# x staged in eight buffers, squares summed on VectorE, and columns of scales turned into rows on TensorE

## The chip, the cores and the metric

The kernel runs on one core of one Trainium2 chip. The metric is device time in microseconds (us), the median of several runs; lower is better. Engine names are those of the profile: PE is TensorE (PEld its weight load), DVE VectorE, ACT ScalarE, POOL GpSimd, and SP the engine that issues nearly all DMAs, in the order of its instructions.

## The reference

The reference is one layer of a hybrid encoder on x, 1024 tokens of width 1024, in float32:

```python
h = rmsnorm(x, norm_g[l])                 # x * rsqrt(mean(x*x) + eps) * g
u = h @ w_in[l]                           # 1024 -> 5312 columns, split for the three mixers and a gate
y_conv = conv_module(...)                 # GLU, depthwise conv of 31 taps, LayerNorm, SiLU
y_ret  = retention_branch(...)            # 4 heads, two directions, chunks of 128
y_mla  = mla_branch(...)                  # rmsnorm of two latents, 8 heads, dense softmax attention
y = jnp.concatenate([y_conv, y_ret, y_mla], axis=-1) * jax.nn.silu(u_gate)
x = x + y @ w_out[l]
return rmsnorm(x, final_g)
```

Four scales are a mean over the width turned into one number per token: rsqrt of the mean square of x, of the query latent and of the key-value latent, and rsqrt of the conv's variance. The softmax sums are one number per token and head.

## The kernel before

Activations lie with features on the 128 partitions and tokens along a row. Each matrix product is made of three matmuls of split operands (high part times high, low times high, high times low: lines 175 to 177, helper `mm3`). A Python program issues work in an order of its own, and a scheduler of the framework then interleaves the streams; each engine runs its instructions in one fixed order, and SP's DMA issues too.

**Prologue (0 to 60 us).** `load_x` brings x in 8 tiles of 128 x 1024 (k = 0 to 7) into tag `hp`, which has four buffers; ACT makes the high part xH, DVE the low part xL (line 63, inside `split_l`), and PE multiplies them with the first weight unit. `sq_x` squares a tile in place on ACT and adds it to the sum `cm` (the tile `ssx`): six adds on POOL, the last on DVE (`SQD`). So the tile of k = 4 to 7 comes in only when the add of k - 4 has freed its buffer.

**Scales of tokens.** `row_rsqrt` (four calls: `cm`, `lss`, `lsk`, `va`) sums over the partitions with eight matmuls of one column against ones (line 300). The stationary operand there takes every eighth token, `ss.rearrange("p (q n) -> p n q", n=KT)[:, n, :]`, so that token p*8 + n ends at partition p, column n. DVE scales the 128 x 8 column (line 301), POOL takes the power (302), SP writes it to memory (303: `r_dram`, `lq_dram`, `lk_dram`, `cr_dram`) and reads it back on all partitions as a row (305, `rbc` for x). For x a column layout `rcol` is read back too (308). PE runs on meanwhile with the next projection unit; the results of the units wait in PSUM for `rbc`, since DVE's evictions multiply by it.

**Projections, conv, retention (60 to 540 us).** PE runs projection units back to back; DVE does the evictions, the weight splits and the 31 conv taps.

**Attention (540 to 990 us).** 16 units (8 heads by two halves of the tokens). A unit makes scores S (lines 810 to 814), row maxima on DVE (817), exponentials with their sums `rs` on ACT (819), transposes of P on PE into the PSUM tag `pp`, which has two banks (828), a copy and a split of them (830, 63), and P times V (175 to 177). `Unit.norm` (833 to 842) takes reciprocals of the 128 x 4 tile `rs`, writes it to memory with `rs_dram<-rs` (839), reads it back as a row on all partitions (841, `rb`) and multiplies the gate with it on POOL. Between the units stand the preparation of the next heads: loads of their weights (`wr`, line 643), the rope turn `xs<-xr` (759), and, late, the output weights `wor` and `yr` (923, 935) for the output projection.

Of the kernel before, what the change touches and what calls it, by code (L numbers as in the profile page):

```python
# [13 lines left out]
ADD, SUB, MUL, MAX = ALU.add, ALU.subtract, ALU.mult, ALU.max  # L14

P = 128
S = 1024
D = 1024
KT = D // P
HS = 512  # L20
CONV_K = 31
HALO = CONV_K // 2
# [8 lines left out]
EPS = 1e-6  # L31
# [14 lines left out]
T18, T19 = 8, 8  # L46
XN = [4, 1, 1, 1, 1, 1, 1, 1]
LASTC = [(0, 0, 256), (1, 0, HS), (0, 256, HS)]
SQD = (7,)
W2_BUFS = 11  # L50
NWARM = 12

# [4 lines left out]
def body(tc, xT, x, w_in, w_uqn, w_uqr, w_uk, w_uv, w_out, vecs, decay, final_g,  # L57
         t_ret, t_mla, t_idx, t_iota, idm, out):
    nc = tc.nc
    act, dve, pool, pe, sp = nc.scalar, nc.vector, nc.gpsimd, nc.tensor, nc.sync  # L60
# [4 lines left out]
    def tt(eng, o, a, b, op):  # L65
        eng.tensor_tensor(o, a, b, op=op)  # L66

    def split_l(eng, lo, src, hi, scale=1.0):
        stt(eng, lo, src, scale, hi.bitcast(F32), MUL, SUB)

    root = ExitStack()
    const = root.enter_context(tc.tile_pool(name="const", bufs=1, side="left"))
# [5 lines left out]
    def ps(tag, w=HS):  # L78
        cnt[0] += 1
        return psp[0].tile([P, w], F32, name=f"ps{cnt[0]}", tag=tag, bufs=PSB[tag])  # L80
# [3 lines left out]
    rr = {"m": 0, "b": 0}  # L84
# [5 lines left out]
    def ps_bg():  # L90
        rr["b"] += 1
        return ps(BG[rr["b"] % len(BG)])

    def mk(pl, shape, dt=F32, tag=None, bufs=None):
        cnt[0] += 1
        kw = {} if bufs is None else {"bufs": bufs}
        return pl.tile(shape, dt, name=f"{tag}{cnt[0]}", tag=tag, **kw)

    r_dram = tc.dram_tile([S], F32, name="r_dram")
# [5 lines left out]
    rcol = mk(const, [P, KT], tag="rcol")  # L105
# [3 lines left out]
    ones = mk(const, [P, P], tag="ones")  # L109
# [11 lines left out]
    rbc = mk(p1, [P, S], tag="rbc")  # L121
# [4 lines left out]
    cv = cvx.enter_context(tc.tile_pool(name="cv", bufs=1, side="right"))  # L126

    ssx = mk(cv, [P, S], tag="cm")

    def load_x(k, n):  # L130
        tf = mk(cv, [P, S + 2 * HALO], tag="hp", bufs=4)[:, :S]
        g = vec[:, V_G + k:V_G + k + 1]
        for i in range(n):
            c = slice(i * S // n, (i + 1) * S // n)
            sp.dma_start(tf[:, c], xT[k * P:(k + 1) * P, c])
            if k == 0 and i == 0:
                pool.dma_start(vec, vecs)
                w0[0][2](0, 1)
            act.activation(xH[k][:, c], tf[:, c], AF.Identity, scale=g)  # L139
            split_l(dve, xL[k][:, c], tf[:, c], xH[k][:, c], g)  # L140
        xraw.append(tf)

    def sq_x(k):
        tf = xraw[k]
        if k == 0:
            act.activation(ssx, tf, AF.Square)
        else:
            act.activation(tf, tf, AF.Square)
            tt(dve if k in SQD else pool, ssx, ssx, tf, ADD)

    xraw = []

    def load_w(u, g, steps=()):
        hi = mk(p1, [P, 4, UW], F32R, tag="wh", bufs=4)
        lo = mk(p1, [P, 4, UW], F32R, tag="wl", bufs=4)
        t = mk(p1, [P, 4, UW], tag="wraw", bufs=2)

        def piece(a, b):
            sp.dma_start(t[:, a:b], w_in[u, g, :, a:b])
            act.copy(hi[:, a:b], t[:, a:b])  # L160
            split_l(dve, lo[:, a:b], t[:, a:b], hi[:, a:b])

        if steps is None:
            return hi, lo, piece
        sp.dma_start(t, w_in[u, g])
        act.copy(hi, t)  # L166
        split_l(dve, lo, t, hi)
        return hi, lo
# [5 lines left out]
    def mm3(o, sh, sl, mh, ml, first, last, skip=False):  # L174
        pe.matmul(o, sh, mh, start=first, stop=False, skip_group_check=skip)  # L175
        pe.matmul(o, sh, ml, start=False, stop=False, skip_group_check=skip)  # L176
        pe.matmul(o, sl, mh, start=False, stop=last, skip_group_check=skip)  # L177
# [88 lines left out]
    for k in range(KT):  # L266
        if k % 4 == 0:
            w0.append(load_w(0, k // 4, None))
        if k == 1:
            w0[0][2](1, 2)  # L270
        elif k > 0 and k % 2 == 0:
            w0[k // 4][2](k % 4, k % 4 + 2)
        load_x(k, XN[k])
        wh, wl = w0[k // 4][0][:, k % 4, :], w0[k // 4][1][:, k % 4, :]
        n = S // 4 if XN[k] == 4 else HS
        for h in range(2):
            for c in range(0, HS, n):
                for t in range(2):
                    c0 = h * HS + c
                    mm3(o4[2 * t + h][:, c:c + n], wh[:, t * P:(t + 1) * P], wl[:, t * P:(t + 1) * P],  # L280
                        xH[k][:, c0:c0 + n], xL[k][:, c0:c0 + n], k == 0 and c == 0, k == KT - 1, True)
        if k > 0:
            sq_x(k - 1)
    sq_x(KT - 1)
    dve.tensor_scalar(cwh, vec[:, V_CW:V_CB], 0.5, None, op0=MUL)
    wn = load_unit(1)

    hps, accs = [], []
    for i in range(NC_CONV):
        hp = mk(cv, [P, S + 2 * HALO], tag="hp", bufs=4)  # L290
# [2 lines left out]
        hps.append(hp)  # L293
        accs.append(mk(cv, [P, S], tag="acc", bufs=4))

    def row_rsqrt(ss, scale, eps, o, d):
        col = mk(const, [P, KT], tag="rrc", bufs=2)
        c = ps_bg()
        for n in range(KT):
            pe.matmul(c[:, n:n + 1], ss.rearrange("p (q n) -> p n q", n=KT)[:, n, :], ones[:, 0:1], start=True, stop=True)  # L300
        dve.tensor_scalar(col, c[:, :KT], scale, eps, op0=MUL, op1=ADD)  # L301
        pool.tensor_tensor(col, col, eps_c[:, :KT], op=ALU.pow)
        sp.dma_start(d.rearrange("(p n) -> p n", n=KT), col)
        if o is not None:
            sp.dma_start(o, d.rearrange("(o s) -> o s", o=1).to_broadcast([P, S]))

    row_rsqrt(ssx, 1.0 / D, EPS, rbc, r_dram)
    sp.dma_start(rcol, r_dram.rearrange("(t p) -> p t", p=P))
    dec = mk(const, [P, 8], tag="dec")
    sp.dma_start(dec, decay.to_broadcast([P, 8]))  # L310
    lg = mk(const, [P, 8], tag="lg")
# [33 lines left out]
    def conv_post():  # L345
        for h in range(2):
            hs = slice(h * HS, (h + 1) * HS)
            o = ps_bg()
            pe.matmul(o, ones, cm[:, hs], start=True, stop=True)
            yield  # L350
            for ci in range(NC_CONV):
                stt(dve, accs[ci][:, hs], o, -1.0 / 512.0, accs[ci][:, hs], MUL, ADD)
                if ci == 0:
                    act.activation(va[:, hs], accs[ci][:, hs], AF.Square)
                else:
                    sq = mk(cv, [P, HS], tag="cb", bufs=2)
                    act.activation(sq, accs[ci][:, hs], AF.Square)
                    tt(dve, va[:, hs], va[:, hs], sq, ADD)
                yield
        row_rsqrt(va, 1.0 / 512.0, EPS, cm, cr_dram)  # L360
        yield
        for ci in range(NC_CONV):
            a = accs[ci]
            tt(dve, a, a, cm, MUL)
            act.activation(a, a, AF.Silu, scale=vec[:, V_LG + ci:V_LG + ci + 1],
                           bias=vec[:, V_LB + ci:V_LB + ci + 1])
            yield
            for h in range(2):
                hs = slice(h * HS, (h + 1) * HS)
                g = mk(cv, [P, HS], tag="cb", bufs=2)  # L370
                sp.dma_start(g, g_dram[ci][:, hs])
                tt(dve, a[:, hs], a[:, hs], g, MUL)
            sp.dma_start(y_dram[ci], a)
            yield
# [42 lines left out]
    def trig(pl, tag):  # L417
        c, s_ = mk(pl, [P, S], tag=tag, bufs=2), mk(pl, [P, S], tag=tag, bufs=2)
        sp.dma_start(c, t_ret[0])
        sp.dma_start(s_, t_ret[1])  # L420
        tt(pool, c, c, rbc, MUL)
        tt(pool, s_, s_, rbc, MUL)
        return c, s_
# [48 lines left out]
    kT[1], qT[1] = mk(rt, [P, 2, S], tag="k1"), mk(rt, [P, 2, S], tag="q1")  # L472
    vN[1] = mk(rt, [P, NCH, UW], tag="v1")
    tr1 = trig(rt, "b4")
    ident = mk(const, [P, P], tag="ident")
    sp.dma_start(ident, idm[0])

    def w2():
        return mk(rt, [P, HS], tag="w2", bufs=W2_BUFS)
# [185 lines left out]
    def half(i):  # L665
        return slice(i * HS, (i + 1) * HS)
# [26 lines left out]
    for h in range(2):  # L693
        t, tk = mk(lx, [P, HS], tag="kr", bufs=2), mk(fin, [P, HS], tag="g" if h else "osb", bufs=2)
# [13 lines left out]
    at = atx.enter_context(tc.tile_pool(name="at", bufs=1, reuse_waits="tile", side="left"))  # L708
# [85 lines left out]
    class Unit:  # L794
# [38 lines left out]
        def norm(self):  # L833
            i = self.h * 2 + self.qh
            self.g = mk(fin, [P, HS], tag="g", bufs=2)
            sp.dma_start(self.g, g_dram[8 + self.h][:, half(self.qh)])
            dve.reciprocal(self.rs, self.rs)
            d = tc.dram_tile([HS], F32, name=f"rs_dram{i}")
            sp.dma_start(d.rearrange("(t p) -> p t", p=P), self.rs)
            rb = mk(fin, [P, HS], tag="rb", bufs=1)  # L840
            sp.dma_start(rb, d.rearrange("(o s) -> o s", o=1).to_broadcast([P, HS]))
            tt(pool, self.g, self.g, rb, MUL)
# [64 lines left out]
    for u in range(NUN):  # L907
# [33 lines left out]
        for i in range(8):  # L941
            cur.qk(i)
            t, j = (i // 2 - 1) % 4, i % 2
# [203 lines left out]
```

## Time and profile before

| | us |
|---|---|
| median of 3 runs | 1168.31 (1164.31 to 1168.86) |
| the profiled execution | 1162.01, span 1160.2 |
| PE busy | 1115.4 (96%) |
| DVE busy | 729.8 (63%) |
| ACT busy | 408.2 (35%) |
| POOL busy | 171.3 (15%) |
| mean granted clock | 0.984 |

PE carries the span. The time that it doesn't work lies in a few places, and a busy PE is slower where the granted clock is below 1, so the profile is read by stage: how much PE idles there, at which clock it runs, and which wait ended last. SP has no busy time of its own; what counts there is the moment at which it issues a DMA.

### The profile page before, as it was taken

How to read it: one execution, taken by the hardware profiler on the slowest of the kernel's cores; microseconds unless marked ns; L12 is line 12 of the kernel's file. 1: busy time of each engine (PE TensorE's matmuls, PEld its weight loads, DVE VectorE, ACT ScalarE, POOL GpSimd, SP SyncE). 2: the span in 40 equal slices, each digit the busy share in tenths (PEclk: the TensorE clock that was granted, in tenths of full speed). 3: DMA queues.
4: the chain of work that ended last, by engine and by line, in shares of the span. 5: the costliest groups of instructions: out<-in, count | busy, mean ns of one | idle time of the engine just before them, and what ended most of it. 6: DMA issues, size and time to landing. Idle time of an engine off the chain costs nothing. (4 is left out here: it accounts for less than half of the span.)

```text
span 1160.2 us, 14263 instructions
## 1 busy us (share of the span) xinstructions
PE 1115.4 (96%) x5548; PEld 933.9 (80%) x5548; DVE 729.8 (63%) x998; ACT 408.2 (35%) x721; POOL 171.3 (15%) x147
## 2 busy tenths in 40 slices
PE   7999999999999999998899999899999979999997
PEld 6888888888898899886678787688778857888886
DVE  6699999997647785746765564555455553345033
ACT  6221222121334134223654453454454443333022
POOL 4300000212220442023201101010110000001000
PEclk9999999998999999999999999999999999999999
DMA  7212223221262122226212212121211242654213
GB/s 261 92 37 73 91 83 117 87 86 46 73 227 91 46 73 69 88 72 227 86 17 74 47 43 53 35 50 35 51 52 29 31 133 56 227 172 150 68 36 109
DMA packets 55491, 101.33 MB, mean 87 GB/s; under 512 B 15584, under 2 KB 19440, under 8 KB 55424
## 3 DMA queue, kind: packets, MB, share of 16 engines
q1 hardware_dynamic: 55376, 100.35, 27.6%
q8 instruction: 43, 0.70, 0.4%
q14 instruction: 24, 0.20, 0.1%
q0 software_dynamic: 48, 0.08, 0.1%
HBM read 74.14 MB, written 24.17 MB: 85 GB/s over the span
## 5 line engine op out<-in xcount | busy, mean ns | idle before, releaser
L176 PE MATMUL ps<-xL,wh 128*128 128x512 f32 (+1 forms) x612 | 240.2, 393 | 3.2 <-DVE xL L63 3.0
L177 PE MATMUL ps<-xH,wl 128*128 128x512 f32 (+1 forms) x612 | 239.6, 392 | 1.9 <-DVE wl L63 1.9
L175 PE MATMUL ps<-xH,wh 128*128 128x512 f32 (+1 forms) x612 | 238.9, 396 | 2.2 <-ACT xH L139 1.6
L63 DVE SCALAR_TENSOR_TENSOR acc<-hp,cwh,acc 128x1024 f32<-128x1024 f32 x120 | 153.3, 1317 | 0.3 <-DVE rrc L301 0.2
L176 PEld LDWEIGHTS ps<-xL,wh 128*128 128x128 f32 x612 | 116.6, 190 | 27.6 <-DVE xL L63 4.2
L177 PEld LDWEIGHTS ps<-xH,wl 128*128 128x128 f32 x612 | 116.1, 190 | 26.5 <-DVE wl L63 2.6
L175 PEld LDWEIGHTS ps<-xH,wh 128*128 128x128 f32 x612 | 116.0, 190 | 26.6 <-ACT xH L139 1.8
L63 DVE SCALAR_TENSOR_TENSOR PL<-ps,PH 128x512 fp32r<-128x512 f32 x128 | 85.7, 685 | 48.7 <-ACT PH L830 48.4
L175 PE MATMUL ps<-woH,yh 128*128 128x512 f32 (+1 forms) x264 | 99.2, 389 | 7.6 <-ACT yh L936 7.4
L176 PE MATMUL ps<-woL,yh 128*128 128x512 f32 (+1 forms) x264 | 101.4, 387 | 0.0
L177 PE MATMUL ps<-woH,yl 128*128 128x512 f32 (+1 forms) x264 | 100.3, 387 | 0.0
L830 ACT CAST PH<-ps 128x512 fp32r<-128x512 f32 x128 | 72.6, 590 | 69.9 <-PE ps L828 69.3
L817 DVE TENSOR_REDUCE nm<-ps 128x1 f32<-128x1024 f32 x64 | 78.1, 1221 | 29.8 <-PE ps L814 29.3
L819 ACT ACTIVATE P<-ps,nm 128x1024 f32<-128x1024 f32 x64 | 71.8, 1122 | 26.3 <-DVE nm L817 24.8
L828 PE MATMUL ps<-ident,P 128*128 128x128 f32 x512 | 73.2, 274 | 4.6 <-DVE PL L63 4.5
L828 PEld LDWEIGHTS ps<-ident,P 128*128 128x128 f32 x512 | 61.5, 141 | 18.0 <-DVE PL L63 6.9
L166 ACT CAST wh<-wraw 128x1024 fp32r<-128x1024 f32 x40 | 42.1, 1051 | 95.0 <-PE ps L176 92.1
L66 POOL TENSOR_TENSOR g<-g,rb 128x512 f32<-128x512 f32 x16 | 20.6, 1289 | 362.2 <-DMA rb<-rs_dram 201.4
L175 PEld LDWEIGHTS ps<-woH,yh 128*128 128x128 f32 x264 | 49.7, 188 | 19.2 <-ACT yh L936 8.4
L63 DVE SCALAR_TENSOR_TENSOR wl<-wraw,wh 128x1024 fp32r<-128x1024 f32 (+2 forms) x45 | 55.4, 1232 | 8.2 <-ACT wh L166 7.4
L177 PEld LDWEIGHTS ps<-woH,yl 128*128 128x128 f32 x264 | 49.7, 188 | 10.8 <-DVE yl L63 0.7
L176 PEld LDWEIGHTS ps<-woL,yh 128*128 128x128 f32 x264 | 49.7, 188 | 10.4
(280 smaller groups left out, 2056.9 us busy)
## 6 DMA issues: line engine op xcount, KB each, us to landing
wraw<-in_w_in_dram SPq DMA_DIRECT2D x40, 512.0 KB, 3.4
wor<-in_w_out_dram SPq DMA_DIRECT2D x16, 512.0 KB, 4.5
g_dram<-ga SPq DMA_DIRECT2D x29, 256.0 KB, 2.0
yr<-y_dram SPq DMA_DIRECT2D x18, 256.0 KB, 4.7
g<-g_dram SPq DMA_DIRECT2D x16, 256.0 KB, 3.4
rb<-rs_dram SPq DMA_DIRECT2D x16, 256.0 KB, 4.9
y_dram<-osb SPq DMA_DIRECT2D x16, 256.0 KB, 2.4
z<-in_x_dram SPq DMA_DIRECT2D x8, 512.0 KB, 3.7
```

What stands on the lines that cost most here:

```text
L63: eng.scalar_tensor_tensor(o, a, s, b, op0=op0, op1=op1)
L66: eng.tensor_tensor(o, a, b, op=op)
L166: act.copy(hi, t)
L175: pe.matmul(o, sh, mh, start=first, stop=False, skip_group_check=skip)
L176: pe.matmul(o, sh, ml, start=False, stop=False, skip_group_check=skip)
L177: pe.matmul(o, sl, mh, start=False, stop=last, skip_group_check=skip)
L817: dve.tensor_reduce(nm, self.S, axis=AX.X, op=MAX, negate=True)
L819: act.activation(p, self.S, AF.Exp, bias=nm, accum_out=self.rs[:, t:t + 1])
L828: pe.transpose(o[:, c * P:(c + 1) * P], self.p[t][:, (4 * j + c) * P:(4 * j + c + 1) * P], ident)
L830: act.copy(ph, o)
```

## The change

1. Tiles k = 4 to 7 of x are staged in tag `acc` (four buffers that the conv uses later), so eight buffers hold the eight tiles. All seven square-adds go to DVE, and the program issues the squares after the loop of loads and splits.
2. `row_rsqrt` takes 128 tokens that lie next to each other as the stationary operand, so the column n holds tokens n*128 to n*128 + 127. The 128 x 8 column is transposed on PE into another part of the same PSUM bank, ACT copies the 8 x 128 result to SBUF, and SP writes 8 rows of 512 bytes instead of 128 of 32. `rcol` is the column itself; its read is gone. The identity for the transposes is loaded at the start.
3. `Unit.norm` transposes `rs` on PE into a `pp` bank, ACT copies the 4 x 128 result, and SP writes 4 rows of 512 bytes instead of 512 elements of 4 bytes.

```diff
     def load_x(k, n):
-        tf = mk(cv, [P, S + 2 * HALO], tag="hp", bufs=4)[:, :S]
+        tf = mk(cv, [P, S + 2 * HALO], tag="hp", bufs=4)[:, :S] if k < 4 else mk(cv, [P, S], tag="acc", bufs=4)
...
             act.activation(tf, tf, AF.Square)
-            tt(dve if k in SQD else pool, ssx, ssx, tf, ADD)
+            tt(dve, ssx, ssx, tf, ADD)
...
-        if k > 0:
-            sq_x(k - 1)
-    sq_x(KT - 1)
+    for k in range(KT):
+        sq_x(k)
...
-    def row_rsqrt(ss, scale, eps, o, d):
-        col = mk(const, [P, KT], tag="rrc", bufs=2)
+    def row_rsqrt(ss, scale, eps, o, d, col=None):
+        if col is None:
+            col = mk(const, [P, KT], tag="rrc", bufs=2)
         c = ps_bg()
         for n in range(KT):
-            pe.matmul(c[:, n:n + 1], ss.rearrange("p (q n) -> p n q", n=KT)[:, n, :], ones[:, 0:1], start=True, stop=True)
+            pe.matmul(c[:, n:n + 1], ss[:, n * P:(n + 1) * P], ones[:, 0:1], start=True, stop=True)
         dve.tensor_scalar(col, c[:, :KT], scale, eps, op0=MUL, op1=ADD)
         pool.tensor_tensor(col, col, eps_c[:, :KT], op=ALU.pow)
-        sp.dma_start(d.rearrange("(p n) -> p n", n=KT), col)
+        pe.transpose(c[:KT, P:2 * P], col, ident)
+        row = mk(cv, [P, HS], tag="cb", bufs=2)[:KT, :P]
+        act.copy(row, c[:KT, P:2 * P])
+        sp.dma_start(d.rearrange("(n p) -> n p", p=P), row)
         if o is not None:
             sp.dma_start(o, d.rearrange("(o s) -> o s", o=1).to_broadcast([P, S]))
 
-    row_rsqrt(ssx, 1.0 / D, EPS, rbc, r_dram)
-    sp.dma_start(rcol, r_dram.rearrange("(t p) -> p t", p=P))
+    ident = mk(const, [P, P], tag="ident")
+    sp.dma_start(ident, idm[0])
+    row_rsqrt(ssx, 1.0 / D, EPS, rbc, r_dram, rcol)
...
             d = tc.dram_tile([HS], F32, name=f"rs_dram{i}")
-            sp.dma_start(d.rearrange("(t p) -> p t", p=P), self.rs)
+            c = ps("pp")
+            pe.transpose(c[:4, :P], self.rs, ident)
+            row = mk(at, [4, P], tag="rr", bufs=2)
+            act.copy(row, c[:4, :P])
+            sp.dma_start(d.rearrange("(t p) -> t p", p=P), row)
             rb = mk(fin, [P, HS], tag="rb", bufs=1)
```

The order of instructions moves at three places. First, SP in the prologue before (line 135 loads x, 159 and 165 weights; the other names are small constants, `xn` the rope tables):

```order
L135 DMA hp_264<-in_xT_dram 128x1024
L159 DMA wraw_260<-in_w_in_dram 128x512
L310 DMA dec_385<-in_decay_dram 128x8
L389 DMA i_1418<-in_idm_dram 128x128
L419 DMA xn_1871<-in_t_ret_dram 128x1024
L420 DMA xn_1872<-in_t_ret_dram 128x1024
L476 DMA ident_2595<-in_idm_dram 128x128
L165 DMA wraw_344<-in_w_in_dram 128x1024
L135 DMA hp_282<-in_xT_dram 128x1024
L135 DMA hp_303<-in_xT_dram 128x1024
L165 DMA wraw_350<-in_w_in_dram 128x1024
L135 DMA hp_321<-in_xT_dram 128x1024
```

and the same place in the changed kernel (x is loaded by line 134 there, weights by 158 and 164):

```order
L134 DMA acc_259<-in_xT_dram 128x1024
L134 DMA acc_275<-in_xT_dram 128x1024
L158 DMA wraw_255<-in_w_in_dram 128x512
L134 DMA acc_294<-in_xT_dram 128x1024
L134 DMA acc_310<-in_xT_dram 128x1024
L310 DMA ident_370<-in_idm_dram 128x128
L313 DMA dec_388<-in_decay_dram 128x8
L392 DMA i_1421<-in_idm_dram 128x128
L164 DMA wraw_344<-in_w_in_dram 128x1024
L422 DMA xn_1880<-in_t_ret_dram 128x1024
```

All x tiles now stand ahead of the constants and of the next unit's weights; before, the last three stood behind them.

Second, DVE in the prologue, before (the sum `cm` gets its one add at the end of the prologue) and after the third tile's split:

```order
L63 SCALAR_TENSOR_TENSOR xL_122<-hp_222,vec_102,xH_114 128x1024
L63 SCALAR_TENSOR_TENSOR xL_123<-hp_240,vec_102,xH_115 128x1024
L63 SCALAR_TENSOR_TENSOR wl_259<-wraw_260,wh_258 128x512
L63 SCALAR_TENSOR_TENSOR xL_124<-hp_264,vec_102,xH_116 128x1024
L63 SCALAR_TENSOR_TENSOR wl_259<-wraw_260,wh_258 128x512
```

and in the changed kernel (splits on line 62, adds on line 65):

```order
L62 SCALAR_TENSOR_TENSOR xL_122<-hp_221,vec_102,xH_114 128x1024
L65 TENSOR_TENSOR cm_135<-cm_135,hp_202 128x1024
L62 SCALAR_TENSOR_TENSOR xL_123<-hp_237,vec_102,xH_115 128x1024
L62 SCALAR_TENSOR_TENSOR wl_254<-wraw_255,wh_253 128x512
L65 TENSOR_TENSOR cm_135<-cm_135,hp_221 128x1024
L62 SCALAR_TENSOR_TENSOR xL_124<-acc_259,vec_102,xH_116 128x1024
L65 TENSOR_TENSOR cm_135<-cm_135,hp_237 128x1024
L62 SCALAR_TENSOR_TENSOR xL_125<-acc_275,vec_102,xH_117 128x1024
L62 SCALAR_TENSOR_TENSOR wl_254<-wraw_255,wh_253 128x512
L62 SCALAR_TENSOR_TENSOR xL_126<-acc_294,vec_102,xH_118 128x1024
L65 TENSOR_TENSOR cm_135<-cm_135,acc_259 128x1024
```

The adds stand between the splits now, one for each split or two.

Third, SP in the seventh attention unit before (839 writes the sums, 841 reads them back, 643 are weights of the next heads, 759 their rope turn, 856 and 836 the unit's output and the next gate):

```order
L839 DMA rs_dram_6072<-rs_5806 128x4x1
L841 DMA rb_6074<-rs_dram_6072 128x512
L643 DMA wr_6576<-in_w_uqr_dram 128x384
L759 DMA xs_6047<-xr_6046 32x512 x4
L643 DMA wr_6704<-in_w_uv_dram 128x512
L856 DMA y_dram_91<-osb_6156 128x512
```

and in the changed kernel (844 and 846 for 839 and 841; 644, 760, 861 for 643, 759, 856):

```order
L644 DMA wr_6622<-in_w_uqr_dram 128x384
L760 DMA xs_6081<-xr_6080 32x512 x4
L644 DMA wr_6750<-in_w_uv_dram 128x512
L844 DMA rs_dram_6106<-rr_6109 4x128
L846 DMA rb_6112<-rs_dram_6106 128x512
L861 DMA y_dram_91<-osb_6194 128x512
```

The write and read of the sums moved from ahead of the next heads' loads to behind them; the unit before it has its `xs` ahead of them as well.

## Rows read from the trace of the kernel before

**Rows 1.** Windows: us, busy (instructions) by engine, PE clock, DMA share, GB/s.

```profile
20.00:60.00 40.00, 35.05 (x140) 28.67 (x140) 28.90 (x44) 13.43 (x14) 16.37 (x15) 0.91 0.33 106
60.00:540.00 480.00, 479.47 (x2476) 412.40 (x2476) 378.05 (x497) 120.97 (x210) 77.48 (x61) 0.99 0.27 91
...
590.00:980.00 390.00, 368.29 (x1873) 303.27 (x1872) 211.03 (x300) 183.19 (x339) 42.39 (x33) 0.99 0.22 52
```

**Rows 2.** Waits of PE: us in total, times, longest us.

```profile
PE ps L175 <- ACT yh L936: 7.4, 4, 3.8
PE ps L828 <- DVE PL L63: 4.5, 4, 1.9
PE ps L175 <- ACT xr L756: 4.5, 1, 4.5
...
PE ps L176 <- DVE xL L63: 3.0, 1, 3.0
```

**Rows 3.** Timeline of SP, prologue: start us, us, instruction.

```profile
15.96 3.67 SPq L135 DMA_DIRECT2D hp<-in_xT_dram  x2
```

**Rows 4.** Timeline of POOL, prologue.

```profile
13.38 8.66 POOL L66 TENSOR_TENSOR cm<-cm,hp 128x1024 f32<-128x1024 f32 x3 [11.34 <-ACT hp L148]
```

**Rows 5.** Timeline of DVE, prologue: a split and an add.

```profile
12.37 1.29 DVE L63 SCALAR_TENSOR_TENSOR xL<-hp,vec,xH 128x1024 fp32r<-128x1024 f32 x1 [0.17 <-ACT xH L139]
...
19.76 3.36 DVE L63 SCALAR_TENSOR_TENSOR xL<-hp,vec,xH 128x1024 fp32r<-128x1024 f32 x1
...
41.43 1.23 DVE L66 TENSOR_TENSOR cm<-cm,hp 128x1024 f32<-128x1024 f32 x1
```

**Rows 6.** Timeline of PE: stalls, one-column sums and the slow stretch behind them.

```profile
29.44 0.50 PE L177 MATMUL ps<-xH,wl 128*128 128x512 f32 x1 [1.92 <-DVE wl L63]
...
43.62 3.74 PE L300 MATMUL ps<-ones,cm 128*128 128x1 f32 x16
...
48.46 0.60 PE L177 MATMUL ps<-xH,wl 128*128 128x512 f32 x1
...
51.85 0.42 PE L176 MATMUL ps<-xL,wh 128*128 128x512 f32 x1
```

**Rows 7.** Weight loads of fp32 matmuls by form: busy us, mean ns | idle before.

```profile
L574 PEld LDWEIGHTS ps<-v,w 128*128 128x128 f32 x64 | 10.1, 192 | 0.4
...
L300 PEld LDWEIGHTS ps<-ones,cm 128*128 128x128 f32 x16 | 3.9, 333 | 0.0
```

**Rows 8.** Timeline of PE in the retention, fp32 matmuls in pairs.

```profile
394.40 0.39 PE L574 MATMUL ps<-v,w 128*128 128x128 f32 x2
394.62 0.39 PE L576 MATMUL ps<-Sf,w 128*128 128x128 f32 x2
```

**Rows 9.** Timeline of DVE: the first evictions.

```profile
54.48 1.29 DVE L186 TENSOR_TENSOR ca<-ps,rbc 128x512 f32<-128x512 f32 x2 [6.92 <-DMA rbc<-r_dram]
```

**Rows 10.** DMA issues: KB each, median us to landing.

```profile
rs_dram<-rs SPq DMA_DIRECT2D x16, 2.0 KB, 9.1
...
r_dram<-rrc SPq DMA_DIRECT2D x1, 4.0 KB, 1.4
```

**Rows 11.** Transposes and their copies, grouped by form.

```profile
L828 PE MATMUL ps<-ident,P 128*128 128x128 f32 x512 | 73.2, 274 | 4.6 <-DVE PL L63 4.5
...
L830 ACT CAST PH<-ps 128x512 fp32r<-128x512 f32 x128 | 72.6, 590 | 69.9 <-PE ps L828 69.3
```

**Rows 12.** Waits of SP.

```profile
SPq L841 <- DMA rs_dram<-rs: 138.0, 16, 10.3
...
SPq L839 <- DVE rs L837: 24.4, 16, 7.4
```

**Rows 13.** Timeline of SP in the seventh attention unit.

```profile
737.25 0.37 SPq L839 DMA_DIRECT2D rs_dram<-rs  x1
746.47 0.33 SPq L841 DMA_DIRECT2D rb<-rs_dram  x1
```

**Rows 14.** Windows with the clock after that stall.

```profile
740.00:760.00 20.00, 15.52 (x70) 12.86 (x70) 7.59 (x11) 5.62 (x11) 4.13 (x4) 0.83 0.24 49
```

More of the change, by code (lines that the diff above doesn't have):

```diff
@@ L48 @@
 LASTC = [(0, 0, 256), (1, 0, HS), (0, 256, HS)]
-SQD = (7,)
 W2_BUFS = 11
@@ L474, in body @@
     tr1 = trig(rt, "b4")
-    ident = mk(const, [P, P], tag="ident")
-    sp.dma_start(ident, idm[0])
     def w2():
```

## The prediction

> **What bounds the kernel now.** I first read the windows by stage. From 60 to 540 us PE is busy 479.5 of 480 us, from 20 to 60 us 35.05 of 40 at a clock of 0.91, in the attention 368.3 of 390 [rows 1]. So PE is the bound everywhere, and time can be won only where PE idles, where it runs below full clock, and where an instruction of its own is dear. Then I read PE's waits for the names of the idle places [rows 2], then for each of them the timeline of the engine that released it, back to the engine that started late. The reader is to see three different sources: a chain of DMA issue, POOL and DVE in the prologue, a slow weight load, and a held SP queue in the attention.
>
> **Part 1, the staging of x.** SP reaches the load of tiles 5 and 6 at 15.96 us and needs 3.67 us for the two [rows 3], because their buffers come free only with POOL's adds, which run 2.9 us each (8.66 for three) [rows 4]. On DVE an add is 1.23, a split 1.29; a split of the same size that runs beside POOL's adds takes 3.36 [rows 5]. PE therefore waits 3.0 for xL [rows 2] and 1.9 for wl [rows 6]. After the first of these, from 24.46 on, seven matmuls start 0.43 us apart instead of 0.228, the first of them less, an excess of about 1.3; the mean clock of 0.91 over 35 us of work bears it out, since 0.09 x 35 = 3.2 is about this and the 1.6 of part 2 [rows 1]. In the new order the loads of all x tiles stand ahead of the constants and wait for nobody, and POOL has no add. DVE gets six more adds, 6 x 1.23 = 7.4 us, and six of 2.9 us leave POOL. Setting the new DVE order one behind the other from the split of tile 2 at 12.37 with 1.29 for a split, 0.68 for a half weight split and 1.23 for an add, xL of tile 7 is ready at about 25.6 and the last add ends near 32; PE, at four groups of three matmuls a tile (12 x 0.228 = 2.7 us), comes to tile 4 at about 19 and to tile 7's low part at about 27. The adds lie beside PE; cover is thin (1.5 us at the end), and if DVE is late by more, PE waits that much. I take the whole: 3.0 + 1.9 + 1.3 = **6.2 us off**; the bounds are 0 (DVE is late again) and 6.4.
>
> **Part 2, row_rsqrt.** The sum over the partitions costs PE 3.74 us for 16 records [rows 6], 0.234 each, and their weight loads 333 ns against 192 ns for fp32 weights that lie next to each other [rows 7]. Those run in pairs 0.22 us apart [rows 8], 0.11 a record. If the stride of eight is all that sets the two apart, a call costs 16 x 0.112 = 1.79 and saves 1.95; if only the loads' durations scale, 3.74 x 192/333 = 2.16 and saves 1.58. I take the first, which is a measured pitch: 4 x 1.95 = **7.8 us off** (bounds 6.3 and 7.8; 0 if the stride is not the reason).
> Behind each call the next matmuls run at half speed: from 48.46 to 51.85 eight of them in 3.39 us [rows 6] where 8 x 0.228 = 1.82 is normal, 1.57 lost; behind the call for `va` I read 1.44 in the same way, and behind `lss` and `lsk`, which stand together, 1.57. The granted clock there is at its lower level, 1.2 GHz. What stood before was 3.7 us of one-column matmuls, as 3.0 us of idling stood before the slow stretch at 24.46; behind the idle of 1.92 at 29.44 [rows 6] the timeline has full speed. A call of 1.8 us is nearest to that case, two in a row (3.6) to the other. So **3.0 us off** (1.57 + 1.44; bounds 0 and 4.6).
> The way through memory gets longer in steps: a transpose, an ACT copy, a DMA of 8 rows. Its first user is DVE's eviction at 54.48, behind a wait of 6.92 [rows 9]. The sum comes some 7 us earlier here (36.7 for 43.62); with the power at 40.7, the transpose behind 28 matmuls at 45.0, the copy, the write (1.4 as before, [rows 10]) and the read the row lands near 51, and PE needs the first evicted bank near 53.7. So 2 to 3 us of cover stay; were it gone, PE would wait that time once. Four transposes at 0.27 at most [rows 11], 0.11 in sequence, are 0.4 us on PE. DVE isn't full in 60 to 540 (378 of 480, [rows 1]), so what PE wins early isn't lost there as long as the conv's end stays ahead of its readers.
> Parts 1 and 2 together: 6.2 + 7.8 + 3.0 - 0.4 = **16.6 us off**.
>
> **Part 3, the softmax sums.** `rs_dram<-rs` takes 9.1 us for 2 KB, written as 512 elements of 4 bytes; `r_dram` takes 1.4 for 4 KB in 128 pieces [rows 10]. SP's next instruction reads the row back and waits for that write: 138 us in 16 waits [rows 12]. All that is queued behind it is late too. In the seventh unit the write goes at 737.25, the read at 746.47 [rows 13], and the weights `wr` stand behind it; ACT waits for them, and PE 4.5 for `xr`, which comes next on ACT [rows 2]. The clock then falls, 0.83 over 15.5 us of work [rows 14]: 0.17 x 15.5 = 2.6, and counted start by start in the timeline 2.4. In the same way stand xs (PE's 4.5 for PL) and the output weights (7.4 for yh); the stretch behind the longest of those loses another 1.6 by the same count. These add up to 4.5 + 4.5 + 7.4 + 2.4 + 1.6 = 20.4 us. Two things in the new order help: the write is in 4 pieces, and it stands behind the next heads' loads. How long the new write takes the trace does not show: the bounds are 1.4 and 9.1, and I take the value near 1.4, whose pieces are nearer in kind (rows of several elements).
> The Trainium skill speaks against it: by "DMA: Bandwidth & Descriptors", section "Rules for kernel authors", an outermost dimension of size c below 16 confines a DMA to at most c engines, here 4, and 8 in part 2. The same list says that a non-contiguous last dimension lowers to one descriptor per element, which the row of 9.1 us agrees with. No run here shows the first; if it made the new write as slow as the old, the sum would be that of the first rival.
> New on PE are 16 transposes (16 x 0.11 = 1.8, at most 16 x 0.27 = 4.4), on ACT 16 copies of 128 columns (the copy of 512 takes 0.59, [rows 11]), and one of the two `pp` banks is held from the transpose to the end of its copy, in which the transposes of P have one bank only. That bound is from 0 to 16 x 0.59 = 9.4; I take 5, the middle. So 20.4 - 1.8 - 5 = **13.6 off**.
>
> **Sum.** 16.6 + 13.6 = 30.2. Against the profiled execution (1162.0, span 1160.2) this is 1131.8. The median before, 1168.3, lies 6.3 above that execution, so in medians the forecast is 1168.3 - 30.2 = 1138.1.
>
> **Rivals.**
> *The attention keeps its stalls.* The new write is as slow as the old, or the waits named go to the ACT copy, P and the bank: the 16.6 stay and 1.8 is paid, 1168.3 - 14.8 = 1153.5. For it: ACT and DVE already alternate tightly there, and only 4.5 + 2.4 of the 20.4 are followed step by step to the held queue. Against: 138 us of SP waiting.
> *The stride isn't the reason for 333 ns.* The form with one moving column could be slow in itself: then 7.8 and 3.0 stay, 1138.1 + 10.8 = 1148.9. For it: no other row has one column. Against: the duration is that of the weight load, whose shape is the same.
> *DVE is late.* With 7.4 us more in the prologue the splits, or the conv's taps behind them, hold PE, and parts 1 and 2 give nothing net: 1138.1 + 16.6 = 1154.7. For it: DVE is the busiest beside PE, and the cover at tile 7 is 1.5 us. Against: the slow splits were slow beside POOL.
> *Slower: PE waits for the column.* In before SP alone waits for the reciprocals, 24.4 us in 16 waits [rows 12], 1.5 a unit. The transpose now stands in PE's own queue; where the scheduler puts it ahead of the last exponential's end, PE waits in place of SP, the scores and PV behind it wait too, and a bank of `pp` stays taken. All other gains are 16.6 + 20.4 - 1.8 = 35.2, so it decides from 35.2 / 16 = 2.2 us a unit. With 1.5 for the reciprocal and 1.0 more for the bank and copy it is 16 x 2.5 = 40, or 1168.3 + 4.8 = 1173.1. Against: only 0.18 us of DVE lies between the last sum and the reciprocal, and the transpose stands among score matmuls of the next unit.
>
> **Chances.** Forecast 0.55; attention unchanged 0.16; stride not the reason 0.09; DVE late 0.08; slower 0.05; several of these at once, so that little is left, 0.07. A difference of 0.5% (5.8 us) is about what a measurement of this kernel can tell from none. The first four are faster by more: 0.88; the mixtures count as within 0.5%: 0.07; slower 0.05. The range: its low end is the sum with no cost for the bank, 1133.1, less 1.6 for the third slow stretch of part 2, less the 5.3 us of the attention's idle that I left out (390 - 368.3 = 21.7, less 16.4), less 4.0 by which the lowest run of before lies under its median: 1122. Its high end takes in the rivals to 1155 and a part of their mixtures: 1160.
>
> **What would show it.** In the changed kernel's profile: no wait of PE for xL or wl between 20 and 30 us, and DVE splits of 1.3; one-column sums of about 1.8 us with weight loads near 192 ns; full clock behind the first and the last of them; `rbc` landing near 51 without a new wait of PE; `rs_dram` landing in about 2 us and SP's waits for it below 40 us in sum; PE's waits for xr and yh gone. The forecast is wrong if PE's waits for PL, or for rs, grow past 15 us, if the sums still take 3.7, or if DVE releases new waits in the prologue.

## The result and the profile after

The changed kernel takes 1125.46 us (median of 4 runs, 1123.56 to 1128.17) against 1168.59 before (1164.31 to 1169.04): a ratio of 0.9646, 95% interval 0.9621 to 0.967, so 43.1 us off where 30.2 were forecast. It lies inside the range of 1122 to 1160, near its low end. Its profiled execution took 1124.83, span 1123.0, at a mean clock of 0.992.

I cut both spans at the start of the same pieces of work on PE: the sum over partitions for `cm`, that for `lss`, the first product of the retention, and the first and the last transpose of P. The windows of the kernel before (columns as in [rows 1]):

```profile
0.00:43.60 43.60, 35.84 (x162) 29.19 (x163) 33.64 (x48) 24.64 (x31) 17.57 (x21) 0.96 0.60 204
43.60:259.80 216.20, 216.20 (x948) 179.53 (x948) 203.39 (x193) 42.33 (x56) 16.54 (x9) 0.99 0.25 83
259.80:384.80 125.00, 125.00 (x640) 108.81 (x640) 82.20 (x126) 33.47 (x58) 28.62 (x17) 0.96 0.31 102
384.80:573.50 188.70, 180.02 (x1050) 156.49 (x1049) 126.21 (x222) 65.17 (x131) 51.28 (x47) 0.98 0.31 101
573.50:987.70 414.20, 392.49 (x2012) 324.09 (x2010) 225.44 (x320) 197.41 (x367) 46.50 (x36) 0.99 0.21 50
987.70:1160.20 172.50, 165.89 (x744) 135.75 (x742) 58.93 (x91) 45.16 (x82) 10.81 (x18) 0.99 0.37 128
```

and of the changed kernel:

```profile
0.00:36.90 36.90, 34.77 (x162) 29.75 (x163) 27.78 (x45) 24.66 (x31) 1.80 (x15) 1.00 0.70 248
36.90:249.70 212.80, 212.80 (x948) 176.41 (x948) 200.34 (x200) 42.34 (x55) 16.92 (x9) 1.00 0.25 83
249.70:369.80 120.10, 120.10 (x644) 103.48 (x643) 86.65 (x129) 34.21 (x61) 31.05 (x17) 0.97 0.32 106
369.80:559.50 189.70, 180.57 (x1051) 156.50 (x1050) 125.61 (x222) 64.86 (x131) 52.87 (x48) 0.98 0.31 100
559.50:950.10 390.60, 386.48 (x2027) 321.41 (x2025) 226.71 (x320) 201.24 (x382) 45.38 (x35) 1.00 0.17 53
950.10:1123.00 172.90, 165.97 (x745) 135.74 (x742) 59.26 (x91) 45.60 (x83) 11.18 (x18) 0.99 0.37 128
```

The reader is to subtract window from window: 6.7 us off to the first sum, 3.4 and 4.9 in the next two, 1.0 and 0.4 given back in the fourth and sixth, 23.6 off in the attention. That is 37.2, the difference of the spans.

The answers to [rows 2] and [rows 12], PE's longest waits of the attention and SP's at the softmax sums:

```profile
PE ps L174 <- DVE kL L62: 2.8, 4, 1.0
...
PE ps L811 <- ACT qH L747: 0.7, 2, 0.3
PE ps L811 <- ACT P L820: 0.7, 1, 0.7
```

```profile
SPq L844 <- ACT rr L843: 127.6, 15, 17.9
...
SPq L846 <- DMA rs_dram<-rr: 15.7, 16, 2.9
```

PE's waits for yh, PL and xr are gone. SP still stands for 127.6 us at the sums, now in front of the write; only the wait behind the write shrank, from 138.0 to 15.7, and both waits together come to 143.3 where they were 162.4. In SP's timeline the write and the read that answer to [rows 13] are 1.2 us apart:

```profile
709.57 0.27 SPq L844 DMA_DIRECT2D rs_dram<-rr  x1
710.79 0.33 SPq L846 DMA_DIRECT2D rb<-rs_dram  x1
```

For [rows 5], [rows 6] and [rows 9], DVE's and then PE's timeline:

```profile
20.11 1.28 DVE L62 SCALAR_TENSOR_TENSOR xL<-acc,vec,xH 128x1024 fp32r<-128x1024 f32 x1
...
23.11 1.21 DVE L65 TENSOR_TENSOR cm<-cm,acc 128x1024 f32<-128x1024 f32 x1
...
50.74 1.29 DVE L185 TENSOR_TENSOR ca<-ps,rbc 128x512 f32<-128x512 f32 x2 [10.86 <-DMA rbc<-r_dram]
```

```profile
36.95 1.84 PE L299 MATMUL ps<-ones,cm 128*128 128x1 f32 x16
38.65 0.48 PE L176 MATMUL ps<-xH,wl 128*128 128x512 f32 x1
38.97 0.39 PE L174 MATMUL ps<-xH,wh 128*128 128x512 f32 x1
```

No split is slow, the sum takes 1.84 instead of 3.74, the matmuls behind it run at full speed, and the row lands in time for an eviction at 50.74. In nine traces of kernels with this prologue the sum starts between 36.5 and 38.5, and in the two with the prologue of before at 43.6 and 46.4. The weight loads of that call (ns: min/median/max) are those of [rows 7] for neighbouring tokens:

```profile
L299 PEld LDWEIGHTS ps<-ones,cm x16: 188/192/192, 36.7 to 38.5; 128*128 128x128 f32 x16
```

Behind the pair of calls for the latents the slow stretch is still there, and longer: thirteen matmuls from 253.85 to 259.47 in 5.62 us, where 13 x 0.228 = 2.96 is normal.

```profile
251.44 2.54 PE L299 MATMUL ps<-ones,lsk 128*128 128x1 f32 x16
253.85 0.77 PE L174 MATMUL ps<-xH,wh 128*128 128x512 f32 x1
...
259.11 0.52 PE L174 MATMUL ps<-xH,wh 128*128 128x512 f32 x1
259.47 0.39 PE L175 MATMUL ps<-xL,wh 128*128 128x512 f32 x1
```

### The profile page after: what moved, and what is told of

The parts are those of the page before. It is cut to its first block, busy times and chain, and to the rows that moved or that the text cites. A ratio compares the mean times of both kernels' runs of the same rounds, so it can differ in the third digit from the quotient of the medians.

```text
span 1123.0 us, 14301 instructions
## 1 busy us (share of the span) xinstructions
PE 1100.7 (98%) x5568; PEld 923.3 (82%) x5568; DVE 726.4 (65%) x1004; ACT 412.9 (37%) x741; POOL 159.2 (14%) x141
## 4 chain that ended last, share of the span: by engine, by line
PE 94%; DVE 2%; DMA 1%; ACT 1%; issue 1%; SPq 0%; POOL 0%; POOLq 0%; DVEq 0%; ACTq 0%
PE ps L174 24%; PE ps L175 24%; PE ps L176 24%; PE ps L829 4%; PE ps L811 3%; PE ps L815 3%; PE ps L814 3%; PE ps L813 3%; PE ps L812 3%; PE ps L299 1%; PE ps L575 1%; PE ps L564 1%; PE ps L579 1%; PE ps L577 1%; DMA hp<-in_xT_dram 1%
## 5 line engine op out<-in xcount | busy, mean ns | idle before, releaser
L175 PEld LDWEIGHTS ps<-woL,yh 128*128 128x128 f32 x264 | 49.6, 188 | 10.4
L174 PEld LDWEIGHTS ps<-woH,yh 128*128 128x128 f32 x264 | 49.6, 188 | 10.4
L176 PEld LDWEIGHTS ps<-woH,yl 128*128 128x128 f32 x264 | 49.6, 188 | 10.3
```

## The experiments

Ratios are to the kernel before on the same chip. The kernel before itself ran between 1159.4 and 1168.9 (medians) on the chips used, so where times of different groups of runs are subtracted, the ratios are the safer comparison. The changed kernel, run again beside three of the others, took 1123.77 (1122.34 to 1127.24), ratio 0.9636 (0.9609 to 0.9663).

**Is part 3 the attention's gain?** `e1_old_sums` undoes it:

```diff
-            c = ps("pp")
-            pe.transpose(c[:4, :P], self.rs, ident)
-            row = mk(at, [4, P], tag="rr", bufs=2)
-            act.copy(row, c[:4, :P])
-            sp.dma_start(d.rearrange("(t p) -> t p", p=P), row)
+            sp.dma_start(d.rearrange("(t p) -> p t", p=P), self.rs)
```

> The changed kernel with part 3 undone: the softmax sums are written from the 128 x 4 tile as 512 elements of 4 bytes, with no transpose and no copy, and the scheduler puts the write and the read ahead of the next heads' loads again. If part 3 gives what the two traces show between the first and the last transpose of P (23.6 us of the 37.2), the time is about 1125 + 24 = 1149, with PE's waits for xr, yh and PL back (some 16 us). If the stalls of the attention went because the earlier stages end sooner, the time is about 1126 to 1130.

Measured: 1145.5 (1143.05 to 1145.91), ratio 0.9799 (0.9761 to 0.9838). The stalls are back, with SP's wait:

```profile
PE ps L174 <- ACT yh L937: 4.4, 3, 2.7
PE ps L174 <- ACT xr L757: 4.2, 1, 4.2
...
PE ps L829 <- DVE PL L62: 4.0, 4, 1.7
```

```profile
SPq L842 <- DMA rs_dram<-rs: 138.1, 16, 10.9
```

So part 3, and not the earlier end of the other stages, frees the attention: 20 to 22 us against either median of the changed kernel, 18 to 19 through the ratios (0.9799 against 0.9646 and 0.9636).

**Length or place of the write?** Part 3 makes the write short and also moves it behind the next heads' loads. Two kernels part the two. `e5_short_direct` has the write early and short:

```diff
-            c = ps("pp")
-            pe.transpose(c[:4, :P], self.rs, ident)
-            row = mk(at, [4, P], tag="rr", bufs=2)
-            act.copy(row, c[:4, :P])
-            sp.dma_start(d.rearrange("(t p) -> t p", p=P), row)
+            sp.dma_start(d.rearrange("(p t) -> p t", t=4), self.rs)
```

> The write stands early in SP's order as before, but is short: the 128 x 4 tile goes out as 128 rows of 16 bytes, with no transpose and no copy (the row comes out in another order of tokens, so the factors meet the wrong tokens). If the length of the write is what held SP, the write takes 1.5 to 2.5 us, PE's stalls stay away and the time is 1122 to 1127. If the order is what counts, the stalls come back though the write is short: about 1140 to 1149.

Measured: 1122.66 (1121.15 to 1124.33), ratio 0.9609 (0.9571 to 0.9646). The write takes 2.0 us, PE has no wait for yh or xr, and SP's waits at the sums are

```profile
SPq L842 <- DMA rs_dram<-rs: 30.6, 16, 3.1
SPq L840 <- DVE rs L838: 29.7, 16, 7.4
```

`e4_long_write` has it late and long:

```diff
-            sp.dma_start(d.rearrange("(t p) -> t p", p=P), row)
+            sp.dma_start(d.rearrange("(p t) -> t p", t=4), row)
```

> The write stands late in SP's order as in the changed kernel, with transpose and copy, but is long: the 4 x 128 row is written to places 16 bytes apart, as 512 elements of 4 bytes (the row comes out in another order of tokens). If the length of the write is what held SP, SP's read waits some 9 us again in each unit and the time is about 1140 to 1149. If the order is what counts, nothing that PE needs soon stands behind it and the time is 1124 to 1130.

Measured: 1244.82 (1241.48 to 1247.11), ratio 1.0651 (1.0607 to 1.0696), far above both expectations. One place of it, on POOL, DVE and PE in turn:

```profile
788.58 1.26 POOL L65 TENSOR_TENSOR g<-g,rb 128x512 f32<-128x512 f32 x1 [14.32 <-DMA rb<-rs_dram]
```

```profile
789.87 0.69 DVE L65 TENSOR_TENSOR osb<-ps,g 128x512 f32<-128x512 f32 x1 [8.90 <-POOL g L65]
790.48 0.68 DVE L62 SCALAR_TENSOR_TENSOR PL<-ps,PH 128x512 fp32r<-128x512 f32 x1
```

```profile
791.22 1.12 PE L829 MATMUL ps<-ident,P 128*128 128x128 f32 x4 [6.99 <-DVE PL L62]
```

The write is issued at 775.79 and the read 8.2 us later; the gate's multiply waits for the row, DVE's `osb` for the gate, and the next split PL stands behind `osb` in DVE's queue, so PE waits 7 us. In all DVE waits 144.6 us for the gate (16.9 in the changed kernel) and PE 54.8 for PL:

```profile
DVE osb L65 <- POOL g L65: 144.6, 16, 15.3
PE ps L829 <- DVE PL L62: 54.8, 11, 7.0
```

Of the rest, PE waits 23.1 us for kL (2.8 in the changed kernel), and the mean clock of this execution is 0.950. So length is what counts, at either place, and the late place is the worse one for a long write: it is the schedule that suits a short one. The Trainium skill ("DMA: Bandwidth & Descriptors", "Rules for kernel authors") has one descriptor per element for a last dimension that isn't contiguous; the runs agree, 9.1 and 8.2 us for 512 pieces, 2.0 for 128, 1.2 for 4. (9.1 and 2.0 are medians to landing, 8.2 and 1.2 the time from the write's issue to that of the read which waits for it.) What the Trainium skill has in the same section of at most c engines for an outermost dimension of c cost nothing that can be seen here: the 4-row write is the shortest of them.

**Is the stride the reason for the slow sums?** `e2_strided`:

```diff
-            pe.matmul(c[:, n:n + 1], ss[:, n * P:(n + 1) * P], ones[:, 0:1], start=True, stop=True)
+            pe.matmul(c[:, n:n + 1], ss.rearrange("p (q n) -> p n q", n=KT)[:, n, :], ones[:, 0:1], start=True, stop=True)
```

> The changed kernel with the stationary operand of the sums over partitions at a stride of eight again, all else as changed (so the scales meet the wrong tokens). If the stride sets the weight loads' 333 ns, each of the four calls takes 3.7 us again instead of 1.84 and the stretch at half clock is back behind the first and the last: 4 x 1.9 + 3.0 less what the pair's longer slow stretch cost in the changed kernel (about 2), so 1125 + 8 to 11 = 1133 to 1136. If one moving column is what made the loads slow, nothing changes: 1125.

Measured: 1134.93 (1133.98 to 1137.27), ratio 0.9717 (0.9672 to 0.9763), 9.5 to 11.2 above the changed kernel. The weight loads are back at 333 ns (by form: busy us, mean ns | idle before), and the clock is low again behind each call, here at the pair:

```profile
L299 PEld LDWEIGHTS ps<-ones,cm 128*128 128x128 f32 x16 | 3.9, 333 | 0.0
```

```profile
245.00:275.00 30.00, 30.00 (x123) 25.67 (x122) 24.83 (x25) 2.61 (x4) 8.76 (x4) 0.83 0.15 54
```

**What in part 1 removed the stalls?** `e7_pool_adds` undoes only the place of the adds:

```diff
-            tt(dve, ssx, ssx, tf, ADD)
+            tt(dve if k == 7 else pool, ssx, ssx, tf, ADD)
```

`e8_four_bufs` undoes only the buffers:

```diff
-        tf = mk(cv, [P, S + 2 * HALO], tag="hp", bufs=4)[:, :S] if k < 4 else mk(cv, [P, S], tag="acc", bufs=4)
+        tf = mk(cv, [P, S + 2 * HALO], tag="hp", bufs=4)[:, :S]
```

`e3_old_staging` has both of these edits, and the squares inside the loop as before.

> The changed kernel with part 1 undone: x in four buffers, six adds on POOL, squares inside the loop. If part 1 gives what the prologue shows (stalls of 3.0 and 1.9 and the slow stretch of 1.3), PE reaches the first sum over partitions some 6 to 7 us later, at about 43.5, and the time is 1125.5 + 6.5 = 1132. If other slack takes it up later, the time is 1126 to 1128.

> Half of part 1: eight buffers, but six of the seven square-adds on POOL. If the buffers alone removed the stalls, the time is 1125 to 1127. If DVE's splits beside POOL's adds are what held PE (2.7 to 3.4 us instead of 1.3), PE waits for xL and for the sum again, some 4 to 6 us, and the time is 1129 to 1132.

> The other half: four buffers, all adds on DVE, squares behind the loop in the program. If DVE beside POOL was what held PE, the splits stay at 1.3 us and the time is 1125 to 1127. If the late loads of the tiles 5 to 7 were what held it, those still wait for an add and stand behind the constants, PE waits some 2 to 5 us for them, and the time is 1128 to 1131.

Measured, in the order of these three texts: 1128.42 (1128.09 to 1130.99), ratio 0.9667 (0.9636 to 0.9699), for `e3_old_staging`; 1129.32 (1126.62 to 1131.57), ratio 0.9662 (0.9623 to 0.9702), for `e7_pool_adds`; and 1122.15 (1121.05 to 1124.12), ratio 0.9611 (0.9579 to 0.9642), for `e8_four_bufs`, 3 us under its expectation, which nothing here explains. With eight buffers and the adds on POOL, the loads of tiles 4 and 5 and of 6 and 7 are out by 10 us, and yet:

```profile
15.60 5.95 POOL L65 TENSOR_TENSOR cm<-cm,hp 128x1024 f32<-128x1024 f32 x2
```

```profile
13.86 2.66 DVE L62 SCALAR_TENSOR_TENSOR xL<-hp,vec,xH 128x1024 fp32r<-128x1024 f32 x1 [0.71 <-ACT xH L138]
16.45 2.90 DVE L62 SCALAR_TENSOR_TENSOR wl<-wraw,wh 128x512 fp32r<-128x512 f32 x1
19.27 4.56 DVE L62 SCALAR_TENSOR_TENSOR xL<-acc,vec,xH 128x1024 fp32r<-128x1024 f32 x2
```

```profile
22.69 0.80 PE L175 MATMUL ps<-xL,wh 128*128 128x512 f32 x1 [3.08 <-DVE xL L62]
```

Beside POOL's adds a split takes 2.66 us instead of 1.28 and a half weight split 2.90 instead of 0.68, the split of tile 4 comes behind them, and PE waits 3.08 for it. With four buffers and the adds on DVE, SP still waits at the loads, but the splits are quick and PE has no wait between 18 and 36 us:

```profile
14.96 3.26 SPq L134 DMA_DIRECT2D hp<-in_xT_dram  x2
```

```profile
23.40 1.28 DVE L62 SCALAR_TENSOR_TENSOR xL<-hp,vec,xH 128x1024 fp32r<-128x1024 f32 x1
```

So it was the adds beside DVE, not the buffers: with four buffers in both, the adds on POOL cost 6.3 us (`e3_old_staging` against `e8_four_bufs`, which also differ in where the squares stand). With the adds on DVE the eight buffers bring nothing that can be measured. The first sum of `e8_four_bufs` starts at 39.1, but its delay arises earlier than the held loads: PE's wait for xH ahead of 10.6 us is 2.0 long, and the clock from 10 to 20 us is 0.83, as it is in the changed kernel's second trace (38.5). With the adds on POOL the first sum comes at 40.8 with eight buffers and at 43.6 with four, a difference that the medians don't show.

**Part 3 alone, on the kernel before.** `e11_sums_only` makes the third edit of the diff and no other.

> Part 3 alone, on the kernel before. Undone singly from the changed kernel, part 1 gave 3.8 us (the mean against its two medians), part 2 10.3 and part 3 20.9, together 35.0 of 43 to 44. If the parts are independent, part 3 alone gives 20.9 too, about 1147, and parts 1 and 2 together the rest, 22 to 23, so that those two overlap. If part 3 is worth more on the kernel before, the time is about 1139 (1168 - 29).

Measured: 1142.44 (1139.11 to 1144.61) beside 1159.42 for the kernel before, ratio 0.9848 (0.9822 to 0.9873), 17.0 us. From the first transpose of P to the last it takes just what the changed kernel takes:

```profile
577.10:967.70 390.60, 386.83 (x2027) 321.29 (x2025) 225.80 (x320) 201.16 (x382) 46.93 (x36) 1.00 0.17 53
```

So part 3 gives 23.6 us in the traces by itself. Its median shows less, 17.0, or 1.52% of the kernel before; undoing it costs 1.53% or 1.63% through the ratios, so added alone and undone singly it is worth the same. The three parts undone singly come to about 35 (3.8 + 10.3 + 20.9) of 43 by the medians, and to 29 to 32 by the ratios. I can't place the rest; the trace of this run reaches its first sum at 46.4 where the trace of before, with the same prologue, has 43.6, so a single trace is uncertain by some 3 us there.

**Beyond the changed kernel.** `e6_apart` moves the sum for `lss` one unit ahead; `e10_direct` writes the softmax sums as 128 rows of 16 bytes, with no transpose and no copy, and reads the row in its order of tokens on POOL; `e9_direct_apart` does both.

```diff
     for u in range(8, 11):
-        wn = run_unit(u, wn, ev_lat(2 * (u - 8)), u + 1, 2)
...
-    for ss, n, d in ((lss, 384.0, lq_dram), (lsk, 256.0, lk_dram)):
-        row_rsqrt(ss, 1.0 / n, EPS, None, d)
+        hook = (lambda: row_rsqrt(lss, 1.0 / 384.0, EPS, None, lq_dram)) if u == 10 else None
+        wn = run_unit(u, wn, ev_lat(2 * (u - 8)), u + 1, 2, hook)
+    row_rsqrt(lsk, 1.0 / 256.0, EPS, None, lk_dram)
...
+            sp.dma_start(d.rearrange("(p t) -> p t", t=4), self.rs)
...
-            tt(pool, self.g, self.g, rb, MUL)
+            gv = self.g.rearrange("p (t q) -> p t q", t=4)
+            tt(pool, gv, gv, rb.rearrange("p (q t) -> p t q", t=4), MUL)
```

> The changed kernel once more, as the standard for the three beside it: 1123 to 1128.

> The changed kernel with the sums of the query latent moved one unit earlier, so that PE has 60 and more projection matmuls between them and those of the key-value latent. In the changed kernel the two calls stand in a row, the second runs at half clock in its last part (2.54 for 1.84 us) and 13 matmuls behind it too (2.7 us lost). If two calls in a row are what lowers the clock, both go and the time is 3 us less, 1120 to 1124. If a call by itself lowers it there, nothing changes.

> The softmax sums go out directly as 128 rows of 16 bytes, with no transpose, no copy and no bank, and POOL reads the row back in the order of tokens (a view with a step of 16 bytes in its multiply). If the length of the write is all that counts, it is as fast as the run with the tokens out of order, 2 to 4 us under the changed kernel: 1121 to 1124. If the stepped read slows POOL or, beside it, DVE (16 multiplies of 1.3 us), it is 1125 to 1130.

> Both of the last two together. If they are independent, the gains add up: 5 to 7 us under the changed kernel, 1118 to 1121.

Measured, beside 1123.77 for the changed kernel: 1121.6 (1118.73 to 1123.7), ratio 0.9612 (0.9585 to 0.9639); 1122.01 (1119.92 to 1122.89), ratio 0.9613 (0.9587 to 0.9638); 1119.94 (1119.18 to 1121.58), ratio 0.9599 (0.9573 to 0.9624). Singly each is about 2 us quicker with ranges that overlap; both together are 3.8 us quicker than the changed kernel and their range lies below its own, less than the 5 to 7 expected. POOL's multiply with the stepped read takes 1.58 us instead of 1.32, and nobody waits for it. With the calls apart the stretch around them is at full clock:

```profile
245.00:275.00 30.00, 30.00 (x139) 24.25 (x138) 26.09 (x29) 4.35 (x7) 9.93 (x5) 1.00 0.16 53
```

The same window has 0.89 in the changed kernel's first trace, 0.94 in its second, and 1.00 in `e5_short_direct`, where the two calls stand in a row as well. Of the nine traces with two quick calls in a row, the clock fell behind them in eight, for different lengths, and not in that one; with the calls apart it didn't fall there in the two traces taken.

## Why the prediction was right, and where its sizes were off

**Part 1 (6.2 forecast).** The two traces give 6.7 to the first sum (with the scatter above it can be 5 to 10), and the new DVE order ran as set down: the last split ends at 25.5 (25.6 forecast), the sum starts at 36.95 (36.7). The step "because their buffers come free only with POOL's adds" named the wrong half of the cause. The late loads were true, but they held nobody; the splits beside POOL's adds did, which the same paragraph put second. That the size came out is luck in so far as the change takes away both halves: with the buffers alone, in `e7_pool_adds`, a stall of 3.08 stays. Undone, part 1 costs 3.0 to 4.7 us by the medians: in the traces the 6.7 by which `e3_old_staging` is late at the first sum are 3.3 at its end (span 1126.3), since the stretches from the sum for `lss` to the first transpose of P are 3.7 shorter there.

**Part 2 (10.4 forecast).** The stretch from the first sum to the retention is 8.3 us shorter in the traces, and undoing the stride costs 9.5 to 11.2. A call takes 1.84 for 1.79 forecast, and the slow stretches behind the first and last are gone. Of the 2.1 that the trace lacks, 1.8 are the pair: its slow stretch was kept at 1.57 in the sum, and cost 2.66 behind the pair and 0.7 within it.

**Part 3 (13.6 forecast, 23.6 measured).** This is the mis-sized term, and three of its numbers were too careful. The 5 us for the bank of `pp` were nothing: PE's wait for PL is gone, and at the 16 transposes themselves it waits 0.2 us:

```profile
L841 PE MATMUL ps<-ident,rs 128*4 128x128 f32 x16 | 4.3, 271 | 0.2 <-DVE PL L62 0.2
```

PE's idle time from the first transpose of P to the last fell from 21.7 to 4.1, by 17.6, where the waits named came to 16.4. And its busy time fell by 6.0, where the forecast had 4.0 from the slow stretches less 1.8 for the transposes, 2.2. The slow stretches themselves were counted rightly: summed over windows of 2 us, one minus the granted clock times PE's busy time is 4.2 us in the kernel before and nothing in the changed one, in line with the mean clocks of 0.99 and 1.00 above. So 3.6 us of busy time, 6.0 + 1.8 - 4.2, went at full clock. A part of it lies beside the stalls, by an estimate: PE's waits in this stretch fell from 18 to 7, and the last matmul ahead of a wait counts as busy for its whole 0.39 us instead of the 0.228 to the next start, 11 x 0.16 = 1.8; the rest is not placed. Together 5 for the bank, 1.2 of idle time and 3.8 of busy time are the 10.0 between 13.6 and 23.6. The argument for the place in SP's order was wrong: an early short write is as good.

**Through memory.** `rbc` was forecast near 51 and its first eviction starts at 50.74; PE has no wait for it.

**From the trace to the median.** 37.2 of the 43.1 us are in the two traces. The forecast took the distance of 6.3 us between the execution shown and the median for a constant; but after the change it is 0.6 (1124.83 to 1125.46). The kernel before showed 0.984 as its clock in the profile and 0.972 to 0.985 in its 36 runs beside the experiments, 28 of them at or below 0.981; the changed kernel 0.990 to 0.994 in nine runs, 0.992 in the profile. So its profile was one of the quick ones, with fewer slow stretches than its usual run, and the change took away several of the stalls in front of such stretches. That the remaining 5.9 us are this is argued from the clocks, not shown.

**The rivals.** The attention didn't keep its stalls; the stride was the reason; DVE was not late; and PE didn't wait for the column. What did come near the mechanism of the slower rival is the kernel with the long write at the late place, though by another way, over the gate and DVE's queue.

## What to carry to other kernels

A DMA of a few kilobytes was priced here by its pieces and not by its bytes, and its price is paid by everything queued behind the next instruction that waits for it; make its rows of several elements, if need be by writing them in the order in which they lie and reading them in another, before spending a transpose. Read a slow instruction's neighbours on the other engines before its own inputs: here an add on POOL more than doubled a split on DVE, and buffers were not the matter. And when a stall goes, count what goes with it: compare the busy time of the whole stage as well as its idle time, and take the share of the slow clock out of it by the granted clock, since not all of that fall is the clock.

## What the runs showed of the hardware

A 128 x 128 fp32 weight load takes 192 ns from neighbouring tokens and 333 ns at a stride of eight. A write of 2 KB takes 9.1 us in 512 pieces from 128 partitions, 8.2 in 512 from 4, 2.0 in 128 pieces, and 1.2 to the next issue in 4. A split of 128 x 1024 on DVE took 1.28 us alone and 2.7 to 3.4 beside an add on POOL. The granted clock fell to its lower level, 1.2 GHz, behind the same two calls in eight of nine traces, for different numbers of matmuls: thirteen in one trace of the changed kernel, seven in its second, and none in that of `e5_short_direct`.
